# Six of sixteen feature blocks of a shift and scale moved from TensorE matmuls to VectorE dot products

## The chip, the cores and the metric

One core of one Trainium2 chip. Times are device microseconds (us) of one execution. The kernel before ran three times: 1409.14 us median, 1408.57 to 1409.15. Profile and trace come from one further execution.

## What is computed

One layer of a diffusion backbone for two groups of 128 tokens each (s = 0 prompt, s = 1 sample), model width 2048, feed-forward width 8192, all in float32. Cut to what matters here:

```python
def ada_mod(cvec, w_ada, b_ada):
    m = jax.nn.silu(cvec) @ w_ada + b_ada        # w_ada: 2048 x 12288
    return jnp.split(m, 6, axis=-1)
...
sh1, sc1, g1, sh2, sc2, g2 = ada_mod(c, w_ada, b_ada)
h = rms_norm(x, norm1_w) * (1 + sc1) + sh1       # then h @ w_in, two attentions, their branches, w_out
x = x + g1 * merged
h2 = rms_norm(x, norm2_w) * (1 + sc2) + sh2
x = x + g2 * (relu(h2 @ w_up) ** 2 @ w_down)
```

`c` is one vector per group, so the shift and scale are matrix-vector products with two vectors: 2048 inputs, 2048 outputs each. The change touches `sh2` and `sc2` alone. They are first needed when the second norm is applied, long after their weights can be had.

## The kernel before, in words

**Steps.** The big products run as 456 steps. A step is one weight tile of 512 KB (256 input rows by 512 columns, held as 128 partitions x 1024). For each step SyncE (SP) issues the load of `raw`; ScalarE (ACT) copies it to a rounded high part `wH` (L71, called from L193); VectorE (DVE) subtracts to get the low part `wL` (L206); TensorE (PE) does 12 matmuls of 128x512: high x high, low x high, high x low, for two 128-row slices and two token groups (L241 to L243, or L338 to L340 in the first 72 steps). A step's load is issued eight steps ahead (`LA` 4 and `RL` 4), its parts are made four steps ahead.

Steps 0 to 71 are the first nine column groups of `w_in`; 72 to 135 the eight gate groups; 136 to 167 the branches `w_br_a` and `w_br_b` (four units n of four plus four steps); 168 to 199 `w_out`; then up and down projections.

**The calendar.** The program is recorded step by step (`run`, L219 to L231), and each engine runs its own instructions strictly in that order. Ahead of step i come the loads due, then the preparation of step i + 4, then the step's matmuls, then whatever functions were put down for i with `at` or `ex`. So what stands behind step i on DVE comes after the `wL` of step i + 4, and the calendar fixes order and not time.

**What else DVE does around the change.** The gate g1 is computed on DVE: `gate_dve` (L949), eight SCALAR_TENSOR_TENSOR of 128x512 every five steps from step 84 to 161 (L953), closed four times by `spread`: ACT copies the sum (`SH`), DVE subtracts (`SL`, L75). Attention lies in steps 68 to 121: query and key norms, softmax sums and normalising on DVE, with small matmuls and transposes on PE (L518, L563, L610, L617, L621). At step 121 ACT applies six sigmoids of 128x1024 (L643). In a branch unit n, DVE multiplies and adds from PSUM (L669, L675, L676), and two steps after the unit PE transposes the result (`tT`, L658), so PE waits there for DVE's L676.

**The shift and scale of the second norm.** Sixteen feature blocks of 128 features. For block fb `pair_load` (L252) brings the shift and scale columns, 2 MB in four loads of 512 KB; `pair_mm` (L258, matmuls L265) does 16 float32 matmuls with the two conditioning vectors padded to 32 columns, in four column strips of the array. After each second block ACT copies the sums (`ada_evac`, L268) and one step later `ada_cols` (L274) turns them by four PE transposes (`ps_sel`, L281), and DVE adds strips and bias (L284 to L291). The blocks stand `SS_GAP` = 3.2 in units that make it 6.4 steps from block to block: steps 74, 80, 86, 93 and so on to 170.

**The pool.** Weights, parts and activations share one pool of `GEN` = 48 tiles of 128x1024 float32. A load into a tile waits until the last reader of the tile's former content is done.

Of the kernel before, what the change touches and what calls it, by code (L numbers as in the profile page):

```python
# [10 lines left out]
F32 = mybir.dt.float32  # L11
F32R = mybir.dt.float32r
BF16 = mybir.dt.bfloat16
AF = mybir.ActivationFunctionType
OP = mybir.AluOpType
AX = mybir.AxisListType

P = 128
D = 2048
KC = D // P  # L20
# [15 lines left out]
LA_OUT = {3: 3, 4: 2, 5: 2, 6: 2, 7: 2, 8: 2}  # L36
RL = 4
G1_AT, G1_GAP = 12, 5
SS_AT, SS_GAP = 2, 3.2
PIECES = [[2 * i, 2 * i + 1] for i in range(8)]  # L40
G2_GAP = 6
CHUNKS = [2, 2, 2, 2, 4, 4]
# [7 lines left out]
def tile_hybrid_step(ctx: ExitStack, tc: tile.TileContext, a):  # L50
    nc = tc.nc
    ctx.enter_context(tc.manual_schedule())
    cp = ctx.enter_context(tc.tile_pool(name="consts", bufs=1))
# [5 lines left out]
    act, dve, pe, pool, sync = nc.scalar, nc.vector, nc.tensor, nc.gpsimd, nc.sync  # L59
# [4 lines left out]
    def SM(n, name):  # L64
        return sp.tile([P, 32], F32, name=name, tag="s", bufs=14)[:, :n]

    def bank(name, pool_=None):
        return (pool_ or paux).tile([P, 512], F32, name=name, tag="b")
# [14 lines left out]
    baT = cols[:, 32:128].rearrange("p (a k) -> p a k", k=KC)  # L83
    nwT = cols[:, 128:160].rearrange("p (a k) -> p a k", k=KC)
# [87 lines left out]
    def load_at(i, fn):  # L172

        loads.append((i, len(loads), fn))
# [77 lines left out]
    def pair_load(box, nsub, fb):  # L252

        for q in range(4):
            box[fb, q] = G("araw")
            sync.dma_start(box[fb, q], a["w_pair"][nsub, fb][:, 1024 * q:1024 * q + 1024])

    def pair_mm(box, j, fb):  # L258

        if j == 0:  # L260
            box["ps"] = bank("ps_ada")
        for q in range(4):
            raw = box.pop((fb, q)).rearrange("p (k n) -> p k n", k=4)
            for k in range(4):
                pe.matmul(box["ps"][32 * k:32 * k + 32, 256 * j:256 * j + 256], cpad[:, 4 * q + k, :], raw[:, k, :],  # L265
                          start=j == 0 and q == 0, stop=j == 1 and q == 3, tile_position=(0, 32 * k))

    def ada_evac(box, n=512):  # L268
        box["S"] = sp.tile([P, 512], F32, name="S", tag="S", bufs=2)
        copy(box["S"][:, 0:n], box.pop("ps")[:, 0:n])  # L270

    mod = {}

    def ada_cols(box, nsub, k0, nk):  # L274

        if nsub not in mod:
            mod[nsub] = (cp.tile([P, KC, 2], F32, name=f"shT{nsub}"), cp.tile([P, KC, 2], F32, name=f"scT{nsub}"))
        shT, scT = mod[nsub]
        ps = bank("ps_sel")
        for i in range(2 * nk):  # L280
            pe.transpose(ps[:, i * P:(i + 1) * P], box["S"][:, i * P:(i + 1) * P], ident)  # L281
        ks = slice(k0, k0 + nk)
        t = SM(4 * nk, "t")
        dve.tensor_reduce(t.rearrange("p (i m) -> p i m", m=2),  # L284
                          ps[:, 0:2 * nk * P].rearrange("p (i j m) -> p i m j", j=4, m=32)[:, :, 0:2, :],
                          axis=AX.X, op=OP.add)
        tv = t.rearrange("p (k w s) -> p w k s", w=2, s=2)
        for w, dst in ((1, scT), (0, shT)):
            b = baT[:, 3 * nsub + w, ks].unsqueeze(2).to_broadcast([P, nk, 2])
            dve.tensor_tensor(dst[:, ks, :], tv[:, w], b, op=OP.add)  # L290
        dve.scalar_tensor_tensor(scT[:, ks, :], scT[:, ks, :], 1.0,  # L291
                                 nwT[:, nsub, ks].unsqueeze(2).to_broadcast([P, nk, 2]), op0=OP.add, op1=OP.mult)

    hH, hL = [None] * 4, [None] * 4

# [62 lines left out]
    def mod_pair(f):  # L358

        box, k0 = {}, 2 * f  # L360
        if f == 0:
            for j in range(2):
                pair_load(box, 0, j)
            for fn in [lambda: pair_mm(box, 0, 0), lambda: pair_mm(box, 1, 1), lambda: x_scale(0, 0, 2),
                       lambda: ada_evac(box), lambda: prep_hi(wsteps[0]), lambda: ada_cols(box, 0, 0, 2),
                       lambda: make_h(0, 2), lambda: prep_lo(wsteps[0], 0), lambda: split_h(0, 2),
                       lambda: prep_lo(wsteps[0], 1), lambda: x_scale(0, 2, 4)]:
                pre_at(0, fn)
            return
        i = ADA_AT[f]  # L370
        for j in range(2):
            load_at(i, lambda j=j: pair_load(box, 0, k0 + j))
            at(i, lambda j=j: pair_mm(box, j, k0 + j))
        at(i, lambda: ada_evac(box))
        at(i + 1, lambda: ada_cols(box, 0, k0, 2))
        at(i + 2, lambda: make_h(k0, 2))
        at(i + 3, lambda: split_h(k0, 2))
# [252 lines left out]
    t = 0  # L630
    for mix, s, g in [("A", 0, 0), ("A", 1, 0), ("A", 0, 1), ("A", 1, 1), ("B", 0, 0), ("B", 1, 0), ("B", 0, 1), ("B", 1, 1)]:
        need = [post_at["kvA", 0] + 6, post_at["qA", g] + 6] if mix == "A" else [
            post_at["kB", g] + 6, post_at["qB", g] + 6, end_of(("vB", g)) + 1]
        t = max([t + JOB_GAP] + need)
# [289 lines left out]
    def ex(i, fn):  # L924
        extra.setdefault(i, []).append(fn)
# [42 lines left out]

    end = sched_gate("g1", 2, s0 + G1_AT, G1_GAP)
    assert end <= br0 + 32, (end, br0)  # L970
    for c in range(8):
        box = {}
        for j in range(2):
            i = s0 + SS_AT + int((4 * c + 2 * j) * SS_GAP)
            load_at(i, lambda box=box, c=c, j=j: pair_load(box, 1, 2 * c + j))
            ex(i, lambda box=box, c=c, j=j: pair_mm(box, j, 2 * c + j))
        ex(i, lambda box=box: ada_evac(box))
        ex(i + 1, lambda box=box, c=c: ada_cols(box, 1, 2 * c, 2))
# [33 lines left out]
def _layout(x):  # L1012

    def tiles(w, n=512):
        k, m = w.shape
        return w.reshape(k // 256, 2, P, m // n, n).transpose(0, 3, 2, 1, 4).reshape(k // 256, m // n, P, 2 * n)

    out = {n: x[n] for n in ("x_prompt", "x_sample", "b_ada", "q_norm_a", "k_norm_a", "q_norm_b", "k_norm_b", "sink_a",
                             "cache_a_v", "cache_b_v")}
    for n in ("w_in", "w_br_a", "w_br_b", "w_out", "w_up", "w_down"):  # L1020
        out[n] = tiles(x[n][0])
    out["xT"] = np.stack([x["x_prompt"][0], x["x_sample"][0]]).reshape(2, P, 4, 4, P).transpose(2, 4, 3, 0, 1).reshape(4, P, 1024)
    rows = np.concatenate([x["c_ctx"], x["c"][0], x["b_ada"][0], x["norm1_w"][0], x["norm2_w"][0]])
    out["cols"] = rows.reshape(160, P).T
    ada = x["w_ada"][0]
    out["w_gate"] = np.stack([tiles(ada[:, p * D:(p + 1) * D]) for p in (2, 5)])
    pairs = []
    for p in (0, 3):
        w = ada[:, p * D:(p + 2) * D].reshape(KC, P, 2, KC, P)
        pairs.append(w.transpose(3, 1, 0, 2, 4).reshape(KC, P, KC * 2 * P))  # L1030
    out["w_pair"] = np.stack(pairs)
    out["cache_a_kT"] = x["cache_a_k"][0, 0].transpose(2, 1, 0)
    out["cache_b_kT"] = x["cache_b_k"][0, 0].transpose(2, 1, 0)
    q, k = np.arange(P)[:, None], np.arange(P)[None, :]
    rpb = x["rpb_b"][0]
    dr = k // GRID_W - q // GRID_W + rpb.shape[1] // 2
    dc = np.clip(k % GRID_W - q % GRID_W + rpb.shape[2] // 2, 0, rpb.shape[2] - 1)
    out["rpb_qk"] = rpb[:, dr, dc].transpose(1, 0, 2).reshape(P, NH * P)
    return {n: np.ascontiguousarray(v) for n, v in out.items()}
# [19 lines left out]
```

## Time and profile before

| | |
|---|---|
| median of 3 runs | 1409.14 us (1408.57 to 1409.15) |
| the profiled execution | 1408.84 us, of it the traced span 1407.1 us |
| PE busy | 1395.7 us, 99% of the span |
| DVE busy | 958.5 us, 68% |
| ACT busy | 640.6 us, 46% |
| HBM read | 346.28 MB, mean 249 GB/s |
| the block matmuls L265 (both norms) | 1024 records, 61.2 us |
| the preparation L206 on DVE | 455, mean 1221 ns |
| the gate's L953 on DVE | 256, mean 745 ns |

Busy time is time in which an instruction of the engine is in its recorded span. PE's spans overlap by design, so what a matmul costs is read from the distance of one start to the next. DVE's spans overlap by some 0.09 us where nothing waits; there too the start-to-start distance is the price. A wait is listed with the instruction that ended it.

### The profile page before, as it was taken

How to read it: one execution, taken by the hardware profiler on the slowest of the kernel's cores; microseconds unless marked ns; L12 is line 12 of the kernel's file. 1: busy time of each engine (PE TensorE's matmuls, PEld its weight loads, DVE VectorE, ACT ScalarE, POOL GpSimd, SP SyncE). 2: the span in 40 equal slices, each digit the busy share in tenths (PEclk: the TensorE clock that was granted, in tenths of full speed). 3: DMA queues.
4: the chain of work that ended last, by engine and by line, in shares of the span. 5: the costliest groups of instructions: out<-in, count | busy, mean ns of one | idle time of the engine just before them, and what ended most of it. 6: DMA issues, size and time to landing. Idle time of an engine off the chain costs nothing.

```text
span 1407.1 us, 18890 instructions
## 1 busy us (share of the span) xinstructions
PE 1395.7 (99%) x7118; PEld 1131.3 (80%) x7118; DVE 958.5 (68%) x1272; ACT 640.6 (46%) x846; POOL 48.7 (3%) x65
## 2 busy tenths in 40 slices
PE   8999999999999999999999999999999999999998
PEld 5777778877788777888888888888888888888887
DVE  3677766887776888755747778788754554544754
ACT  3633443365545543344644444444453543425431
POOL 0000010320000000000000000000000000000000
PEclk7999999999999999999999999999999999999999
DMA  9998876778788999975466766767666575565733
GB/s 379 399 364 326 318 290 226 251 250 292 242 288 294 392 339 346 326 232 173 154 222 220 256 226 230 250 239 269 216 203 195 179 209 186 175 209 167 224 109 114
DMA packets 98939, 350.94 MB, mean 249 GB/s; under 512 B 11616, under 2 KB 12640, under 8 KB 98848
## 3 DMA queue, kind: packets, MB, share of 16 engines
q1 hardware_dynamic: 97776, 348.31, 71.9%
q0 software_dynamic: 928, 1.34, 0.3%
q8 instruction: 56, 0.92, 0.3%
q14 instruction: 35, 0.29, 0.1%
q10 hardware_dynamic: 144, 0.08, 0.0%
HBM read 346.28 MB, written 3.41 MB: 249 GB/s over the span
## 4 chain that ended last, share of the span: by engine, by line
PE 98%; issue 1%; ACT 0%; DVE 0%; POOL 0%; POOLq 0%; ACTq 0%
PE acc L241 24%; PE acc L243 24%; PE acc L242 24%; PE acc L338 5%; PE acc L340 5%; PE acc L339 5%; PE ps_ada L265 4%; PE ps_T L658 1%; PE ps_S L563 1%; PE ps_g L940 1%; PE acc L742 1%; PE acc L741 1%; PE acc L740 1%; PE ps_sel L281 1%; PE acc L758 0%
## 5 line engine op out<-in xcount | busy, mean ns | idle before, releaser
L206 DVE TENSOR_TENSOR wL<-raw,wH 128x1024 fp32r<-128x1024 f32 x455 | 537.9, 1221 | 258.7 <-ACT wH L71 251.3
L71 ACT ACTIVATE wH<-raw 128x1024 fp32r<-128x1024 f32 x456 | 460.3, 1054 | 216.8 <-PE acc L243 62.9
L953 DVE SCALAR_TENSOR_TENSOR gacc<-araw,cpad,gacc 128x512 f32<-128x512 f32 x256 | 175.0, 745 | 0.0
L338 PE MATMUL acc<-wH,hH 128*128 128x512 f32 x288 | 114.1, 396 | 2.3 <-ACT hH L71 2.3
L340 PE MATMUL acc<-wH,hL 128*128 128x512 f32 x288 | 113.0, 393 | 0.0
L339 PE MATMUL acc<-wL,hH 128*128 128x512 f32 x288 | 112.8, 392 | 0.0
L241 PE MATMUL acc<-wH,hH 128*128 128x512 f32 x256 | 104.6, 409 | 0.0
L243 PE MATMUL acc<-wH,hL 128*128 128x512 f32 x256 | 100.1, 391 | 0.0
L242 PE MATMUL acc<-wL,hH 128*128 128x512 f32 x256 | 100.0, 390 | 0.0
L830 ACT ACTIVATE up<-acc 128x512 f32<-128x512 f32 x32 | 18.9, 590 | 153.2 <-PE acc L243 145.5
L901 DVE TENSOR_TENSOR dsum<-dsum,acc 128x512 f32<-128x512 f32 x48 | 32.4, 686 | 57.4 <-PE acc L243 57.4
L338 PEld LDWEIGHTS acc<-wH,hH 128*128 128x128 f32 x288 | 54.5, 189 | 16.4 <-issue 2.9
L340 PEld LDWEIGHTS acc<-wH,hL 128*128 128x128 f32 x288 | 54.5, 189 | 11.9 <-DVE hL L75 0.4
L339 PEld LDWEIGHTS acc<-wL,hH 128*128 128x128 f32 x288 | 54.4, 189 | 10.9
L265 PE MATMUL ps_ada<-araw,cpad 128*32 128x256 f32 x1024 | 61.2, 386 | 0.0
L241 PEld LDWEIGHTS acc<-wH,hH 128*128 128x128 f32 x256 | 48.1, 188 | 12.7 <-issue 3.4
L243 PEld LDWEIGHTS acc<-wH,hL 128*128 128x128 f32 x256 | 48.0, 188 | 10.4
L242 PEld LDWEIGHTS acc<-wL,hH 128*128 128x128 f32 x256 | 48.2, 188 | 9.9 <-issue 1.0
L265 PEld LDWEIGHTS ps_ada<-araw,cpad 128*32 128x32 f32 x1024 | 31.0, 111 | 27.4 <-issue 6.0
L71 ACT ACTIVATE S<-ps_ada 128x512 f32<-128x512 f32 x16 | 9.6, 601 | 92.8 <-PE ps_ada L265 92.8
L241 PE MATMUL acc<-wH,h21H 128*128 128x512 f32 x120 | 47.4, 395 | 0.0
L243 PE MATMUL acc<-wH,h20L 128*128 128x512 f32 x120 | 46.8, 390 | 0.0
(477 smaller groups left out, 2791.8 us busy)
## 6 DMA issues: line engine op xcount, KB each, us to landing
raw<-in_w_in SPq DMA_DIRECT2D x136, 512.0 KB, 5.6
araw<-in_w_pair SPq DMA_DIRECT2D x128, 512.0 KB, 7.5
raw<-in_w_up SPq DMA_DIRECT2D x128, 512.0 KB, 4.3
raw<-in_w_down SPq DMA_DIRECT2D x128, 512.0 KB, 4.2
araw<-in_w_gate SPq DMA_DIRECT2D x64, 512.0 KB, 5.6
raw<-in_w_out SPq DMA_DIRECT2D x32, 512.0 KB, 4.7
raw<-in_w_br_a SPq DMA_DIRECT2D x16, 512.0 KB, 6.8
raw<-in_w_br_b SPq DMA_DIRECT2D x16, 512.0 KB, 5.7
```

Of the source, the lines that this page charges most:

```text
L71: act.activation(out, in_, AF.Copy)
L206: dve.tensor_tensor(st["lo"], st["raw"], st["hi"].bitcast(F32), op=OP.subtract)
L241: pe.matmul(acc[tb], sh, wh[:, k, :], start=f, stop=False)
L242: pe.matmul(acc[tb], sh, wl[:, k, :], start=False, stop=False)
L243: pe.matmul(acc[tb], sl, wh[:, k, :], start=False, stop=l)
L265: pe.matmul(box["ps"][32 * k:32 * k + 32, 256 * j:256 * j + 256], cpad[:, 4 * q + k, :], raw[:, k, :], start=j == 0 and q == 0, stop=j == ...
L338: pe.matmul(acc[tb], sh, wh[:, k, :], start=kt == 0 and k == 0, stop=False)
L339: pe.matmul(acc[tb], sh, wl[:, k, :], start=False, stop=False)
L340: pe.matmul(acc[tb], sl, wh[:, k, :], start=False, stop=last and k == 1)
L830: act.activation(up_r[n][:, s, :], acc, AF.Relu)
L901: dve.tensor_tensor(dsum[n][:, s, :], dsum[n][:, s, :], acc[s], op=OP.add)
L953: dve.scalar_tensor_tensor(box["acc"][:, s, :], raw[:, j, :], cpad[:, 4 * kq + 2 * half + j, s:s + 1], box["acc"][:, s, :], op0=OP.mult, o ...
```

## The change

The last six feature blocks (10 to 15) of the second norm's shift and scale leave TensorE. Their weights are laid out by feature on the host (`w_adaT`: a partition is an output feature, the 2048 inputs lie along the row in two halves h). Both conditioning vectors are broadcast to all partitions, half by half (`crow`, `load_cond`), SiLU is applied there by ACT and DVE, and each output is a DVE `tensor_tensor_reduce`, 128x1024 float32, multiply and add, whose running start is the bias (first half) or the first half's result. In the recorded order each dot is two DVE instructions: the operation itself and one that writes the 128x1 result. Each weight tile serves two dots, one for each token group, two steps apart; a new tile comes every five steps from step 61 to 116 (first half) and 124 to 179 (second half). The ten blocks that stay on TensorE are spread 9.6 steps apart instead of 6.4 (`SS_GAP` 4.8): steps 74, 83, 93, 102, 112, 122, 131, 141, 150, 160.

```diff
-SS_AT, SS_GAP = 2, 3.2
+SS_AT, SS_GAP = 2, 4.8
+FB_DVE, DOT_AT, DOT_GAP = 10, 56, 5
...
+    def load_cond(h):
+        for s in range(2):
+            cB[s, h] = G(f"cB{s}")
+            sync.dma_start(cB[s, h], a["crow"][s:s + 1, 1024 * h:1024 * h + 1024].partition_broadcast(P))
+
+    def silu_cond(s, h):
+        t = G("sgB")
+        act.activation(t, cB[s, h], AF.Sigmoid)
+        dve.tensor_tensor(cB[s, h], cB[s, h], t, op=OP.mult)
+
+    def dot_load(box, fb, w, h):
+        box["raw"] = G("aT")
+        sync.dma_start(box["raw"], a["w_adaT"][w, fb - FB_DVE, h])
+
+    def dot(box, fb, w, h, s):
+        dst = mod[1][w][:, fb, s:s + 1]
+        out = box["raw"] if s else G("junk")
+        dve.tensor_tensor_reduce(out, box["raw"], cB[s, h], 1.0, dst if h else baT[:, 3 + w, fb:fb + 1], OP.mult, OP.add, dst)
...
+    i = DOT_AT
+    for h in range(2):
+        load_at(i - 1, lambda h=h: load_cond(h))
+        for s in range(2):
+            ex(i + s, lambda s=s, h=h: silu_cond(s, h))
+        for fb in range(FB_DVE, KC):
+            for w in range(2):
+                i += DOT_GAP
+                box = {}
+                load_at(i, lambda box=box, fb=fb, w=w, h=h: dot_load(box, fb, w, h))
+                for s in range(2):
+                    ex(i + 2 * s, lambda box=box, fb=fb, w=w, h=h, s=s: dot(box, fb, w, h, s))
+        i += 3
+    ex(i, dot_end)
...
-    for c in range(8):
+    for c in range(FB_DVE // 2):
```

`dot_end` is one small DVE operation that turns the six scales into norm weight times one plus scale. The line that created the result tiles is moved out of `ada_cols`, with no effect on the order.

More of the change, by code (lines that the diff above doesn't have):

```diff
@@ L274, in ada_cols @@
     def ada_cols(box, nsub, k0, nk):
-        if nsub not in mod:
-            mod[nsub] = (cp.tile([P, KC, 2], F32, name=f"shT{nsub}"), cp.tile([P, KC, 2], F32, name=f"scT{nsub}"))
         shT, scT = mod[nsub]
@@ L292, in ada_cols @@
                                  nwT[:, nsub, ks].unsqueeze(2).to_broadcast([P, nk, 2]), op0=OP.add, op1=OP.mult)
+    for n in range(2):
+        mod[n] = (cp.tile([P, KC, 2], F32, name=f"shT{n}"), cp.tile([P, KC, 2], F32, name=f"scT{n}"))
     hH, hL = [None] * 4, [None] * 4
@@ L970, in tile_hybrid_step, with dot_end @@
     assert end <= br0 + 32, (end, br0)
-    for c in range(8):
+    cB = {}
+    def load_cond(h):
[13 more added lines that the diff above has]
+        dve.tensor_tensor_reduce(out, box["raw"], cB[s, h], 1.0, dst if h else baT[:, 3 + w, fb:fb + 1], OP.mult, OP.add, dst)
+    def dot_end():
+        scT = mod[1][1][:, FB_DVE:KC, :]
+        nw = nwT[:, 1, FB_DVE:KC].unsqueeze(2).to_broadcast([P, KC - FB_DVE, 2])
+        dve.scalar_tensor_tensor(scT, scT, 1.0, nw, op0=OP.add, op1=OP.mult)
+    i = DOT_AT
[12 more added lines that the diff above has]
+    ex(i, dot_end)
+    assert i <= end_of(("out", 2)), (i, end_of(("out", 2)))
+    for c in range(FB_DVE // 2):
         box = {}
@@ L1031, in _layout @@
     out["w_pair"] = np.stack(pairs)
+    f0 = FB_DVE * P
+    out["w_adaT"] = np.stack([ada[:, p * D + f0:(p + 1) * D].reshape(2, 1024, KC - FB_DVE, P).transpose(2, 0, 3, 1) for p in (3, 4)])
+    out["crow"] = np.stack([x["c_ctx"], x["c"][0]])
     out["cache_a_kT"] = x["cache_a_k"][0, 0].transpose(2, 1, 0)
```

## The prediction

> **What bounds the kernel now.** I read the page's engine rows first, then the chain of work that ended last, then the groups by line. TensorE (PE) is busy for 99% of the span and the chain lies on it for 98%:
>
> ```profile
> PE 1395.7 (99%) x7118; PEld 1131.3 (80%) x7118; DVE 958.5 (68%) x1272; ACT 640.6 (46%) x846; POOL 48.7 (3%) x65
> PE 98%; issue 1%; ACT 0%; DVE 0%; POOL 0%; POOLq 0%; ACTq 0%
> L206 DVE TENSOR_TENSOR wL<-raw,wH 128x1024 fp32r<-128x1024 f32 x455 | 537.9, 1221 | 258.7 <-ACT wH L71 251.3
> L953 DVE SCALAR_TENSOR_TENSOR gacc<-araw,cpad,gacc 128x512 f32<-128x512 f32 x256 | 175.0, 745 | 0.0
> L265 PE MATMUL ps_ada<-araw,cpad 128*32 128x256 f32 x1024 | 61.2, 386 | 0.0
> ```
>
> So whatever leaves PE comes off the time, as long as the engine that takes it over keeps up in the stretch where it works. The 68% of VectorE (DVE) is a mean over unlike stretches and doesn't answer that.
>
> **What leaves PE.** The timeline of PE around one block of L265 and one set of four transposes (start, duration):
>
> ```profile
> 285.88 0.39 PE L243 MATMUL acc<-wH,hL 128*128 128x512 f32 x1
> 286.19 1.93 PE L265 MATMUL ps_ada<-araw,cpad 128*32 128x256 f32 x32
> 288.06 0.50 PE L241 MATMUL acc<-wH,hH 128*128 128x512 f32 x1
> 288.39 0.40 PE L242 MATMUL acc<-wL,hH 128*128 128x512 f32 x1
> 288.63 0.39 PE L243 MATMUL acc<-wH,hL 128*128 128x512 f32 x1
> ...
> 290.68 0.39 PE L243 MATMUL acc<-wH,hL 128*128 128x512 f32 x1
> 290.92 0.60 PE L281 MATMUL ps_sel<-ident,S 128*128 128x128 f32 x4
> ...
> 291.82 0.40 PE L243 MATMUL acc<-wH,hL 128*128 128x512 f32 x1
> ```
>
> Ordinary matmuls start 0.227 us apart (twelve make a step of 2.72). From 285.88 to 288.63 there are three such distances, 0.68, and the block: 2.75 - 0.68 = 2.07 us. Likewise 291.82 - 290.68 - 0.68 = 0.46 for the transposes. Other blocks give the same 2.07 to 2.08. Six blocks and three sets go: 6 x 2.07 + 3 x 0.46 = **13.8 us**, nearly 1%. The spreading of the other ten costs nothing by itself.
>
> **What DVE gets.** 48 dots of 128x1024, four multiplications like L206, one small operation; it loses three times some 0.5 us of small ones (L284 to L291). No row shows the dot. From below: a TENSOR_TENSOR of that size, 1.13 us from start to start (L206, three of them take 3.50 in the timeline at 457.43), if the result's write is free. From above, near: 1.22 in full, 0.06 for a scalar per partition (L953 at 745 ns against 692 for a TENSOR_TENSOR of the same 128x512, L708), 0.16 for the 128x1 instruction, as the small ones at L290 take, nothing overlapped: 1.44. From above, far: a multiplication and a TENSOR_REDUCE one after the other, 1.13 each (L483 takes 1213 ns), some 2.3. I take 1.13 + 0.06 + 0.10 = **1.29**, nearest to the row of the same shape and engine; 0.10 is the distance by which ACT's accumulator read at L579 moves its next instruction.
>
> [...]
>
> **Where DVE has room.** First half of the dots, steps 61 to 118: the table by stage gives DVE 176.17 us busy in the 223 us from 217 to 440, so 47 are free. 24 dots are 31 us, PE's way through is 6.7 us shorter, two multiplications 2.3: 40. Also `wL` is ready some 8 us before PE needs it there. I take this part as hidden. What hides it is DVE's idle time; without it each dot costs up to 1.29.
>
> First tight place, step 126. Before, the six sigmoids hold ACT up, and `wL` comes just in time (timeline of DVE):
>
> ```profile
> 445.46 2.73 DVE L953 SCALAR_TENSOR_TENSOR gacc<-araw,cpad,gacc 128x512 f32<-128x512 f32 x4
> 449.37 1.23 DVE L75 TENSOR_TENSOR SL<-gacc,SH 128x1024 fp32r<-128x1024 f32 x1 [1.18 <-ACT SH L71]
> 457.43 3.50 DVE L206 TENSOR_TENSOR wL<-raw,wH 128x1024 fp32r<-128x1024 f32 x3 [6.83 <-ACT wH L71]
> ```
>
> The first of these three ends at 458.66, PE starts step 126 at 459.06: 0.40 us of slack. The row of waits runs L953, SH, table load, six sigmoids, `wH`, `wL`. In the changed order two dots (2.58) and two multiplications (2.28) come ahead of that L953, small operations of 0.5 go, and PE gets there 2.07 sooner (two blocks between steps 118 and 125 become one). DVE's idle time between 436 and 445 is 0.36 + 1.25 + 0.26 = 1.87. So L953 ends 2.58 + 2.28 - 0.5 + 2.07 - 1.87 = 4.6 later as PE sees it. ACT's table load (1.28) now comes with the new sigmoids at step 119, while ACT waited 3.44 us for PE anyway, so 3.3 remain. PE waits 3.3 - 0.4 = 2.9.
>
> Second tight place, the branches, from there to the transposes of the last unit (L658), which start at 597.50:
>
> ```profile
> core 0: us, PE busy (x) PEld busy (x) DVE busy (x) ACT busy (x) POOL busy (x), PEclk, DMA share, GB/s
> 457.40:597.50 140.10, 140.10 (x796) 110.31 (x789) 120.76 (x156) 58.71 (x68) 1.92 (x3) 1.00 0.95 351
> ```
>
> DVE is at 86% here, against 68% overall. Its work up to the last L676 by start-to-start distances: 46 preparations at 1.135, 64 of L953 at 0.66, 30 operations of 128x512 at 0.6, two of L75 at 1.14, 1.0 of small ones: 115.8. Room: 140.1 - 115.8 = 24.3. In the changed order 18 dots stand in this stretch, 18 x 1.29 = 23.2; PE passes it two blocks and one set of transposes sooner, 4.6; and twice DVE waits for ACT between L953 and L75 (1.34 each, 2.7), which a late engine can't fill. With the 3.3 it is late by 3.3 + 23.2 + 4.6 + 2.7 - 24.3 = **9.5 us**. The 2.9 of step 126 are part of that, since time lost by PE is time gained by DVE. Behind the late L676 the transposes wait in PE's order, and every matmul of `w_out` behind them. From step 170 on DVE has room again (46.24 of 80 us busy from 600 to 680), too late to give PE anything back.
>
> **Edits that I cost at nothing.** Loads: 24 of 512 KB go, 24 of the same size come, one by one instead of four at a time, and four broadcast ones. DMA share is 0.95 in the tight stretch and bytes per step stay the same: 2 MB in 9.6 steps and 0.5 in 5 make 0.31 MB, 2 in 6.4 made 0.31. Today a weight load is issued 12 to 20 us before ACT reads it and lands in 5.6. ACT: four sigmoids, 4.2 us, against three copies of 0.6, with ACT at 58.71 of 140 in the tight stretch.
>
> **Sum.** 13.8 gained, 9.5 lost: 4.3. The profiled execution took 1408.84 (span 1407.1 and 1.7 around it), the median is 0.3 higher: **1404.5 us**.
>
> **Rivals.**
> 1. *DVE hides all.* For it: 68% mean, `wL` 8 us ahead. Against: the slack of 0.40 and of 3.3 us at two places. 1408.84 - 13.8 = 1395.0. With dots at 1.13 the 20 that count save 3.2 of the 9.5: 1401.3, still the forecast's kind. Chance 0.13 (1395 to 1398).
> 2. *Late loads.* Counted from first write to last read in the recorded order, 48 of the pool's 48 tiles are held at step 83, where it was 40, and loads for steps 89 to 91 then wait one step more; SP's queue is in order, so all behind them wait. Against: the 12 to 20 us. One step, 3.2 us with what lies between, at one or two such places on top of the forecast: 1407.5 to 1411. Chance 0.12.
> 3. *The dot costs 2.3 us* (the slower side). Place: the same two. First half: 24 x 2.3 + 2.3 + 6.7 = 64 against 47 of room and 8 of lead, 9 late; the branches another 18 x 1.0 over the 9.5. Loss 9 + 18 + 9.5 = 36 less 13.8: some 1431. It decides from the dot price at which the gain is gone: 4.3 over 20 dots, 0.21 more, 1.50 us. For it: no row has an accumulator on DVE. [...] Chance 0.16.
> 4. *It doesn't do what it says.* Against: the recorded order has 96 matmuls and 12 transposes fewer. 1409. Chance 0.02.
>
> Forecast: 0.57, from 1399 (dots near 1.13, less waiting) to 1407.5 (1.44: 20 x 0.15 = 3.0 more).
>
> **Chances.** Within 0.2% (2.8 us, about what a measurement here can tell from no change) is 1406.3 to 1412. Faster: 0.51 of the forecast and 0.13. Same: 0.06 of the forecast, 0.10 of rival 2, 0.02. Slower: 0.16 and 0.02 of rival 2. The range 1396.5 to 1411 leaves out rival 3, the ends of 1 and 2.
>
> **What would show it.** Right: L265 with 832 records; the dot's group with two instructions that take 1.29 us together from start to start; PE's waits for DVE at `ps_T` L658 (source L676) and for L206 near steps 126 and 156 to 170, some 9.5 us in all, all of it between 445 and 600; chain shares of DVE above 0%. Wrong: PE without gaps there (rival 1), loads ahead of the gaps (2), dots over 1.5 us (3), or waits already before 440, which I take as hidden.

## The result, and the profile after

The changed kernel takes **1431.43 us** (median; 1430.93 to 1435.95) against 1409.14: ratio 1.016, 95% interval 1.0147 to 1.0173. Slower by 22.3 us, where 4.6 us faster was forecast. The profiled execution is the longest of its four, 1435.95 (span 1434.2); some 3.6 us of that lie ahead of step 0, in code that the change doesn't touch, and are left out below.

The page after, the lines that answer to those of before:

```profile
PE 1396.0 (97%) x6914; PEld 1133.3 (79%) x6914; DVE 1017.8 (71%) x1361; ACT 643.1 (45%) x847; POOL 48.9 (3%) x65
PE 71%; DVE 4%; ACT 2%; issue 2%; DMA 0%; POOL 0%; ACTq 0%; DVEq 0%
L207 DVE TENSOR_TENSOR wL<-raw,wH 128x1024 fp32r<-128x1024 f32 x455 | 537.9, 1219 | 250.5 <-ACT wH L72 236.1
L955 DVE SCALAR_TENSOR_TENSOR gacc<-araw,cpad,gacc 128x512 f32<-128x512 f32 x256 | 174.9, 744 | 0.0
L266 PE MATMUL ps_ada<-araw,cpad 128*32 128x256 f32 x832 | 50.8, 394 | 0.0
```

PE lost 192 block matmuls (1024 to 832), just as forecast, and yet is busy as long as before; busy time doesn't tell why. DVE's mean is 71%, still far from full. The shares of the chain add up to 79% only: it is followed back from the end as far as the copy `T_kB` at 301.82 us and no further. So the 71% of PE are nine tenths of what was followed, against 98% before; DVE, 0% before, has 4%. What ended PE's waits says where to look (engine, line, what it waited for: total us, times, longest):

```profile
PE ps_sel L280 <- ACT S L72: 16.5, 4, 10.1
PE ps_S L565 <- ACT T_kB L72: 5.3, 1, 5.3
...
PE ps_PT L612 <- DVE prob L605: 1.4, 1, 1.4
PE acc L243 <- DVE wL L207: 1.4, 1, 1.4
...
PE ps_T L660 <- DVE g_gA L678: 0.7, 1, 0.7
```

The two waits that were forecast (`wL` L207, `ps_T` L660) are the small ones. The two largest are behind ACT, and neither was in the forecast. The largest, at step 123, on ACT:

```profile
471.91 1.06 ACT L72 ACTIVATE SH<-gacc 128x1024 fp32r<-128x1024 f32 x1 [5.72 <-DVE gacc L955]
472.87 3.88 ACT L645 ACTIVATE g_gB<-g_gB 128x1024 f32<-128x1024 f32 x4
476.66 1.99 ACT L645 ACTIVATE g_gA<-g_gA 128x1024 f32<-128x1024 f32 x2
478.55 1.04 ACT L72 ACTIVATE wH<-raw 128x1024 fp32r<-128x1024 f32 x1
479.49 0.57 ACT L72 ACTIVATE S<-ps_ada 128x512 f32<-128x512 f32 x1
```

and on PE:

```profile
480.12 1.12 PE L280 MATMUL ps_sel<-ident,S 128*128 128x128 f32 x4 [10.05 <-ACT S L72]
480.89 0.78 PE L242 MATMUL acc<-wH,hH 128*128 128x512 f32 x1
481.46 0.63 PE L243 MATMUL acc<-wL,hH 128*128 128x512 f32 x1
481.89 0.63 PE L244 MATMUL acc<-wH,hL 128*128 128x512 f32 x1
...
484.68 0.40 PE L242 MATMUL acc<-wH,hH 128*128 128x512 f32 x1
484.92 0.39 PE L243 MATMUL acc<-wL,hH 128*128 128x512 f32 x1
```

Three things are to be seen. The sums of two blocks (`S`) stand in ACT's order behind `SH` and the six sigmoids of step 121, because the new spacing closes a pair at step 122; before, pairs closed at 118 and 131. `SH` itself is late, since DVE finishes `gacc` late: dots and SiLU stand ahead of it. And behind the gap the matmuls start 0.43 us apart instead of 0.23, until 484.4, at a granted clock of 0.50: this wait costs PE some 2 us more than its own length.

**Accounts.** To place the loss I take the distance from start to start of each two matmuls, subtract the undisturbed one (0.227 for 512 columns, 0.11 for a transpose, 2.07 for a block), and sum by steps; gaps and the matmuls 0.43 us apart are both in it. The table gives it in us over the kernel before. The last column but one is 1409.1, less 13.8 where six blocks have left PE (all but e2), plus the sum; it meets each measured median within some 2 us, so no larger loss lies elsewhere. As 13.8 is taken away in it and is in the sum again, it is no test of the 13.8.

| kernel | 81-99 | 100-117 | 118-126 | 127-170 | sum | worked out | median |
|---|---|---|---|---|---|---|---|
| changed | 9.6 | 8.7 | 14.5 | 4.2 | 37.0 | 1432.3 | 1431.4 |
| e1 no dots | 1.2 | -0.2 | 7.6 | 0.0 | 8.6 | 1403.9 | 1404.3 |
| e2 dots only | 10.4 | 6.6 | 6.2 | 2.3 | 25.5 | 1434.6 | 1436.6 |
| e3 blocks 8 steps later | 14.4 | 7.6 | 11.8 | 5.3 | 39.1 | 1434.4 | 1435.1 |
| e4 old spacing | 10.4 | 6.6 | 6.1 | 12.4 | 35.5 | 1430.8 | 1431.1 |
| e5 first half early | 2.0 | -0.2 | 9.7 | 4.2 | 15.7 | 1411.0 | 1412.2 |
| e6 e5 and e3 | 3.6 | -0.1 | 5.6 | 5.3 | 14.4 | 1409.7 | 1410.1 |
| e7 e6, second half later | 3.6 | -0.1 | 1.5 | 3.8 | 8.8 | 1404.1 | 1404.3 |
| e8 e1 and e3 | 2.3 | -0.1 | 1.5 | 0.0 | 3.7 | 1399.0 | 1399.0 |
| e9 short dots | 6.0 | 3.6 | 11.2 | 0.9 | 21.7 | 1417.0 | 1416.7 |
| e10 one dot later | 9.9 | 7.5 | 14.2 | 4.2 | 35.8 | 1431.1 | 1431.5 |
| e11 second half split | 3.7 | -0.1 | 1.5 | 6.1 | 11.2 | 1406.5 | 1407.3 |
| e12 e9, result buffer | 5.0 | 3.5 | 10.8 | 0.8 | 20.1 | 1415.4 | 1416.9 |
| e13 e9, no loads | 1.4 | 1.7 | 11.0 | 0.1 | 14.2 | 1409.5 | 1409.9 |
| e14 split thin | 3.6 | -0.1 | 1.5 | 1.5 | 6.5 | 1401.8 | 1401.8 |

32.8 of the 37.0 us lie in steps 81 to 126, the attention and its end.

### The profile page after: what moved, and what is told of

Same layout as the page of the kernel before. It is cut to its first block, busy times and chain, and to the rows that moved or that the text cites. A ratio compares the mean times of both kernels' runs of the same rounds, so it can differ in the third digit from the quotient of the medians.

```text
span 1434.2 us, 18598 instructions
## 1 busy us (share of the span) xinstructions
PE 1396.0 (97%) x6914; PEld 1133.3 (79%) x6914; DVE 1017.8 (71%) x1361; ACT 643.1 (45%) x847; POOL 48.9 (3%) x65
## 4 chain that ended last, share of the span: by engine, by line
PE 71%; DVE 4%; ACT 2%; issue 2%; DMA 0%; POOL 0%; ACTq 0%; DVEq 0%
PE acc L242 21%; PE acc L243 21%; PE acc L244 21%; DVE wL L207 2%; PE ps_T L660 1%; ACT wH L72 1%; PE ps_ada L266 1%; PE acc L744 1%; PE acc L742 1%; PE acc L743 1%; PE ps_PT L612 0%; PE ps_S L565 0%; PE acc L760 0%; DVE gacc L955 0%; PE ps_g L942 0%
## 5 line engine op out<-in xcount | busy, mean ns | idle before, releaser
L207 DVE TENSOR_TENSOR wL<-raw,wH 128x1024 fp32r<-128x1024 f32 x455 | 537.9, 1219 | 250.5 <-ACT wH L72 236.1
L243 PEld LDWEIGHTS acc<-wL,hH 128*128 128x128 f32 x256 | 49.5, 193 | 10.4 <-issue 0.5
L266 PE MATMUL ps_ada<-araw,cpad 128*32 128x256 f32 x832 | 50.8, 394 | 0.0
L243 PE MATMUL acc<-wL,h21H 128*128 128x512 f32 x120 | 46.7, 389 | 0.0
L243 PE MATMUL acc<-wL,h20H 128*128 128x512 f32 x120 | 46.7, 389 | 0.0
```

The source lines that it names most:

```text
L207: dve.tensor_tensor(st["lo"], st["raw"], st["hi"].bitcast(F32), op=OP.subtract)
L243: pe.matmul(acc[tb], sh, wl[:, k, :], start=False, stop=False)
```

## Experiments

Two theories at first. A: the new spacing of the blocks is the cause (`S` behind `SH`). B: the dots are, by making DVE late.

**e1 and e2: each part alone.** e1 has the ten spread blocks and no dots:

```diff
-    i = DOT_AT
-    for h in range(2):
...
-    ex(i, dot_end)
+    for w in range(2):
+        dve.memset(mod[1][w][:, FB_DVE:KC, :], 1.0)
```

> Left out: the 48 dots, their 24 weight loads, the broadcast vectors and their SiLU; the shift and scale of blocks 10 to 15 are a constant, so the output is not the reference's. The ten PE blocks stay 9.6 steps apart. Theory A (the new spacing puts the copy of the sums, S, in ACT's order behind the gate's SH and, at step 121, behind six sigmoids, and PE's transposes wait for S): of the 13.8 us saved on PE some 9 are lost again at step 123 alone (S can come no earlier than about 458 on the clock of before, PE is there at about 451, and the matmuls after the gap run at half rate for some 2 us), 1403 to 1406. Theory B (all of the loss is VectorE being late because of the dots): 1395.3, no wait at the transposes.

Measured 1404.34, ratio 0.9955 (0.9938 to 0.9972), with a wait of 5.3 at `ps_sel` in step 123. As A has it: without any dot 8.6 of the 13.8 us are lost again, 7.6 of them in steps 118 to 126. How much of the 8.6 is the new places and how much PE's coming sooner, e1 doesn't tell; e8 below bears on it. Ten blocks at the old spacing without dots were not run. e2 has the dots and all sixteen blocks at their old places:

```diff
-SS_AT, SS_GAP = 2, 4.8
+SS_AT, SS_GAP = 2, 3.2
...
-        dst = mod[1][w][:, fb, s:s + 1]
+        dst = mod[0][w][:, fb, s:s + 1]
...
-    for c in range(FB_DVE // 2):
+    for c in range(8):
```

> All sixteen blocks stay on PE at their old steps, and the 48 dots with loads, broadcast and SiLU are added, their results going where nothing reads them. Theory A (spacing): no transposes behind SH, so the dots alone cost only what DVE is late near steps 126 and 166 to 169, less than the 9.5 us forecast since PE is slower by 13.8: 1411 to 1418. Theory B (dots): 1409.1 + 22.3 + 13.8 = 1445.

Measured 1436.62, 1.0179 (1.0155 to 1.0203). Here A fails: without any spacing the dots cost 25.5 us, where 2 to 9 were expected, though less than B's 36.

**e3 and e4: the blocks elsewhere.** In e3 `SS_AT` is 10 instead of 2, in e4 `SS_GAP` is 3.2 instead of 4.8.

> The changed kernel with its ten blocks eight steps later (82 instead of 74, the same 9.6 apart), so S is copied at steps 91, 110, 130, 149, 168, away from SH at 101, 121, 141, 161; this also gives T_kB another pool tile, long free. Theory A: the waits of 16.5 us at ps_sel and 5.3 at T_kB and the half-rate matmuls behind them (some 6) go: 1403, up to 1409 where DVE's lateness then shows elsewhere. Theory B: DVE is as late as before, the same time is lost at other places: 1427 to 1432.

> The changed kernel with the old spacing for its ten blocks: steps 74, 80, 86 to 131, S copied at 80, 93, 106, 118, 131. Theory A: as in the run with the shifted blocks, 1402 to 1409; PE has its blocks earlier, so less of them lies in the steps where DVE is tight, and DVE is later there by up to 4 us more. Theory B: 1427 to 1435.

Measured 1435.05, 1.0175 (1.0159 to 1.019), and 1431.07, 1.0147 (1.0126 to 1.0169). A fails on both. B's range has e4 in it; e3 lies 3 us above it. The waits at `ps_sel` shrink to 2.5 and 2.1, and others appear in their place, in e3 for instance:

```profile
PE acc L242 <- ACT wH L72: 4.4, 1, 4.4
PE ps_S L565 <- ACT T_kB L72: 3.8, 1, 3.8
PE ps_qT L520 <- ACT probT L72: 2.8, 1, 2.8
PE ps_g L942 <- ACT prob L577: 2.6, 1, 2.6
PE ps_sel L280 <- ACT S L72: 2.5, 2, 1.7
```

So the list of waits of the changed kernel named the nearest place where PE met a late DVE or ACT; with that place gone it meets them at the next. These five end on ACT; the next two, 2.2 each, end on DVE.

**e5 to e8: dots out of the attention.** That led to theory C: not the dots' number but their place inside the attention. If so, the same 24 dots must cost nothing ahead of step 72.

```diff
-    i = DOT_AT
     for h in range(2):
+        i = (20, 119)[h]
...
-                i += DOT_GAP
+                i += (4, 5)[h]
```

> The changed kernel with only the first half of the dots (24 of 48, with their loads and SiLU) moved ahead of the attention: from steps 61 to 118 to steps 24 to 70, every four steps instead of five; the second half (124 to 181) and the blocks stay. Theory C (in the attention, steps 81 to 126, each PE wait is a chain DVE, ACT, PE in strict order, and a dot ahead of a softmax operation delays all of it though DVE has idle time in the mean): the excess of PE's steps over their undisturbed length, 31 us there, falls to the 7 of the run without dots: 1431.4 - 24 = 1407. Theory D (48 dots on DVE cost the same wherever they stand, or their loads delay the weights, DMA being at 0.9 and more before 180 us): 1425 to 1432, with the waits now before step 72.

> As the run with the first half of the dots ahead of the attention, and in addition the blocks eight steps later, so that S is no longer copied behind SH and the sigmoids. Theory C: the remaining 7 to 9 us at the transposes go too; left are the second half's waits between steps 126 and 170, which were 4 to 7 us: 1395.3 + 5 = 1400, range 1397 to 1404. Theory D: 1427 to 1435.

> As the run before it, and in addition the second half of the dots nine steps later (133 to 190 instead of 124 to 181), so that four dots and two SiLU multiplications fewer stand ahead of step 126 and six more behind step 169. Theory C: 1 to 4 us less than the run before it, 1396 to 1400. If the transposes of the last branch unit hold against any delay, nothing.

> Left out: the dots and all that serves them, as in the first run without dots (six blocks' shift and scale are a constant); the ten blocks stand eight steps later, S away from SH. All theories: PE is rid of 13.8 us and nothing waits, 1409.1 - 13.8 = 1395.3. Above 1398 the term of 13.8 or the cause given for the 9 us of the first run is wrong.

e6 adds `SS_AT` 10 to e5; e7 has (20, 128) in place of (20, 119); e8 is e1 with `SS_AT` 10. Measured: e5 1412.15 (1.0018, 1.0006 to 1.003), e6 1410.10 (0.9997, 0.9986 to 1.0009), e7 1404.32 (0.9955, 0.994 to 0.9969), e8 1398.96 (0.9924, 0.9899 to 0.9949). Theory C holds in the main and D falls: e5's excess in steps 81 to 117 drops from 18.3 to 1.8. (Loads, tiles and SiLU moved with these dots; e9 to e13 take them apart.) e5 is still 5 us above C's 1407, with 9.7 left in steps 118 to 126 and 4.2 behind them. The 24 early dots with their 6 MB of loads cost nothing where they now stand. e6 came out 10 us above its expectation: 5.6 are still lost in steps 118 to 126, where SiLU and the first dots of the second half stand ahead of the gate, and 5.3 in the branches. e7, with the second half nine steps later, loses 1.5 and 3.8 there; it gained 5.8 on e6, more than the 1 to 4 expected, and ended 4 above its range. e8 missed its 1395.3 by 3.7, and passed by 1.0 the 1398 above which its expectation called the 13.8 or the cause wrong: PE without its blocks runs into the attention's own chain and into step 126 (`ps_o` waits 1.4 for `prob`, `wL` 0.8). That is the floor for these places of the blocks. So of e1's 8.6 the places make 4.9, as those go when the blocks stand eight steps later.

**e9 to e13: what of the dots costs.** e9 keeps every instruction and load and only shortens the dots.

```diff
-        dve.tensor_tensor_reduce(out, box["raw"], cB[s, h], 1.0,
+        dve.tensor_tensor_reduce(out[:, 0:32], box["raw"][:, 0:32], cB[s, h][:, 0:32], 1.0,
```

> Left out: of each dot all but the first 32 of its 1024 inputs, so each takes some 0.15 us of DVE instead of 1.28; the loads, the pool's tiles, the order of all instructions and the number of instructions stay those of the changed kernel. Theory C (DVE's time inside the attention's chains): as the first run without dots, 1404, up to 1409 with what the loads and the SiLU cost. Theory E (the 24 extra loads and the full pool, with T_kB in the tile of a dot's unused result): the waits stay, 1422 to 1430.

Measured 1416.73, 1.0044 (1.0031 to 1.0058): between both. The dots' time on DVE makes 15.3 of the 37.0 us; 13.1 more than e1 are left with hardly any dot time (0.17 us each from start to start). For those, e10 moves one dot (`i == 81`, s 0) by two steps, e12 gives the unused results a buffer of their own (`out = jk`), e13 also drops the 24 loads.

> The changed kernel with one dot of 48 moved two steps later: the one ahead of T_kB, whose pool tile had held that dot's unused result. T_kB now takes a tile freed by an earlier subtraction. If that tile was the cause of the wait of 5.3 us at step 82, it and some 2 us of half-rate matmuls go, 1424; if DVE is late there anyway, the wait shrinks by the dot's 1.28 or moves on to the next place, 1429 to 1431.

> Left out: all but 32 of each dot's 1024 inputs, as in the run with short dots; in addition the unused results go to a small buffer of their own and no longer take 24 tiles of the pool. If the result tiles made the 13 us that were left: 1404 to 1408. If the loads, the weight tiles or the SiLU did: 1414 to 1417.

> Left out: all but 32 of each dot's inputs, and the 24 weight loads with their tiles; the short dots multiply the broadcast vector with itself. SiLU, broadcast and the order stay. If loads and tiles made the 13 us: 1404 to 1408, what is left above 1404 being the SiLU at steps 119 and 120 (some 3.6 us at step 123). If the SiLU and the small instructions made them: 1414 to 1417.

Measured: e10 1431.45 (1.0152, 1.0129 to 1.0174), e12 1416.90 (1.0056, 1.0041 to 1.0071), e13 1409.93 (1.0006, 0.9997 to 1.0016). So loads with their tiles and the result tiles make 7.5 (e9 to e13); SiLU, the broadcast loads and the small instructions make 5.6 (e13 to e1), of these 3.4 at step 123, where the two new sigmoids and two multiplications stand ahead of `SH`. The result tiles alone make 1.6 in the table (e9 to e12) and nothing in the medians. How the pool acts is seen at step 82. In the changed kernel ACT's `T_kB` waits for the tile that a dot's unused result had held:

```profile
301.82 1.08 ACT L72 ACTIVATE T_kB<-ps_qT 128x512 f32<-128x512 f32 x2 [3.42 <-DVE shT L994]
```

With that dot moved (e10) the copy ahead of it waits for another tile, one being stored to the output:

```profile
297.09 1.06 ACT L72 ACTIVATE wH<-raw 128x1024 fp32r<-128x1024 f32 x1 [3.15 <-DMA out_new_b_k<-u_kB]
298.06 1.06 ACT L72 ACTIVATE T_kB<-ps_qT 128x512 f32<-128x512 f32 x2
```

and PE waits 5.0 instead of 5.3. My guess that this one tile was the cause is wrong; in both cases the tile that came next had been freed a moment before. Without the loads (e13) no wait for `T_kB` is left. Whether loads do harm beyond the tiles that they hold was not separated.

**e11 and e14: a better placing of the second half.** Both are e7 with other steps for the second half's tiles:

```diff
+        steps = iter(([*range(24, 72, 4)], [132, 139, 146, 153, 160, 167, 170, 173, 176, 179, 182, 185])[h])
...
-                i += DOT_GAP
+                i = next(steps)
```

(e14; e11 has 131, 134, 137, 140 and then 167 to 188 in threes.)

> As the run with the first half early and the second half late, but the second half's tiles stand at steps 131 to 140 (four) and 167 to 188 (eight) and none in the branches between. Theory C: the 4 us of waits at the branch transposes and at step 166 go, 1404.3 - 3.5 = 1400.8, and the run without dots at 1399 is the floor; range 1399.5 to 1402.5. If eight tiles in 22 steps are too many for DVE in w_out, waits appear at steps 170 to 199 and it is 1403 or more.

> First half of the dots early (steps 24 to 70), blocks eight steps later, second half thin in the branches and dense behind them: tiles at steps 132, 139, 146, 153, 160 and then every three steps from 167 to 185. DVE's room between steps 126 and 169 takes some 13 dots by the reckoning made ahead of the result, here are 10 or 11: waits at the branch transposes fall from 4 us to under 1, 1404.3 - 3.5 = 1401, floor 1399. If they don't fall, 1404 and the room is smaller than reckoned.

Measured: e11 1407.28 (0.9981, 0.9971 to 0.999), a miss; eight dots in twelve steps make PE wait 3.4 at `ps_T` in step 145, and behind the wait matmuls start 0.43 us apart instead of 0.23, which comes on top. e14 **1401.81** (0.9947, 0.9932 to 0.9962), faster than both kernels. Here are three stretches, roughly up to step 71, up to the tight place at step 126 (123 in the changed kernel) and up to step 170, first before (columns: busy us and instructions of each engine):

```profile
core 0: us, PE busy (x) PEld busy (x) DVE busy (x) ACT busy (x) POOL busy (x), PEclk, DMA share, GB/s
60.00:256.00 196.00, 196.00 (x1161) 154.68 (x1160) 143.20 (x208) 78.01 (x93) 10.92 (x13) 1.00 0.83 305
256.00:460.00 204.00, 203.87 (x1223) 162.02 (x1222) 158.70 (x290) 109.44 (x196) 24.49 (x24) 1.00 0.78 272
460.00:600.00 140.00, 140.00 (x778) 110.93 (x777) 119.42 (x156) 57.98 (x69) 1.92 (x3) 1.00 0.95 349
```

the changed kernel:

```profile
60.00:256.00 196.00, 196.00 (x1161) 154.69 (x1160) 149.51 (x210) 79.67 (x96) 8.97 (x11) 1.00 0.84 310
256.00:480.00 224.00, 200.83 (x1103) 159.60 (x1101) 185.02 (x333) 111.64 (x199) 26.64 (x27) 0.96 0.72 250
480.00:627.00 147.00, 143.62 (x732) 114.82 (x732) 139.05 (x190) 58.53 (x69) 1.91 (x3) 0.98 0.89 328
```

and e14:

```profile
60.00:256.00 196.00, 196.00 (x1161) 154.71 (x1160) 172.11 (x250) 81.59 (x97) 11.88 (x11) 1.00 0.89 332
256.00:460.00 204.00, 200.14 (x1105) 161.00 (x1104) 162.10 (x293) 109.76 (x197) 25.57 (x26) 1.00 0.74 254
460.00:600.00 140.00, 138.80 (x748) 110.64 (x748) 136.10 (x184) 61.65 (x72) 1.91 (x3) 1.00 0.93 345
```

Before step 72 DVE goes to 88% in e14 (172.11 of 196) and PE waits not at all. In the attention DVE is at 83% in the changed kernel (185.02 of 224), with 39 us of it idle, and PE stands still for 23 (224 less 200.83).

## Why the prediction was wrong, point by point

- **What bounds, and what leaves PE: right.** Steps 127 to 170 of e1 test the price: with three blocks and one set of transposes fewer, and no wait there, PE takes 134.58 us against 141.15 before, 6.57 less, where 3 x 2.07 + 0.46 = 6.67 were priced. A slip without effect: the sum leaves out its own last 0.3, since 1409.14 - 4.3 is 1404.8 and not 1404.5.
- **The dot's price: right.** 1.29 was taken, 1.20 measured from start to start as the timeline of DVE shows; the accumulator's read starts together with the next operation, so what it costs lies within the 1.20. On DVE, changed kernel:

```profile
300.44 1.28 DVE L994 CUSTOM_DVE_ANT_0 junk<-aT,cB,cols 128x1024 f32<-128x1024 f32 x1
301.64 0.08 DVE L994 DVE_READ_ACCUMULATOR2_ANT shT<- 128x1 f32 x1
301.64 1.22 DVE L207 TENSOR_TENSOR wL<-raw,wH 128x1024 fp32r<-128x1024 f32 x1
```

  So a dot takes 1.20 us where an L207 of the same size takes 1.13, and not the 2.3 of the far bound.
- **"I take this part as hidden": the step that failed.** Room of 47 us against 40 of work was a sum over 223 us. In steps 72 to 126 much of DVE's idle time is the waiting part of chains: DVE computes a maximum, ACT the exponential, PE a transpose, and so back, each engine in a fixed order. A dot ahead of the maximum delays the whole round, and the idle time behind it can't be used. In the changed kernel, on DVE, ACT and PE, with PE's step 101 starting at 376.34:

```profile
371.86 1.28 DVE L994 CUSTOM_DVE_ANT_0 junk<-aT,cB,cols 128x1024 f32<-128x1024 f32 x1
...
375.33 1.28 DVE L994 CUSTOM_DVE_ANT_0 aT<-aT,cB,cols 128x1024 f32<-128x1024 f32 x1
...
376.54 0.68 DVE L584 TENSOR_REDUCE mx<-ps_S 128x4 f32<-128x512 f32 x1
...
380.03 1.22 DVE L207 TENSOR_TENSOR wL<-raw,wH 128x1024 fp32r<-128x1024 f32 x1 [2.60 <-ACT wH L72]
...
390.50 1.06 ACT L72 ACTIVATE SH<-gacc 128x1024 fp32r<-128x1024 f32 x1 [7.24 <-DVE gacc L955]
...
393.04 1.11 PE L280 MATMUL ps_sel<-ident,S 128*128 128x128 f32 x4 [4.05 <-ACT S L72]
```

  The maximum (`mx`) starts 0.20 us behind the step's start; in e1 it starts 5.47 us ahead of it (361.81 against 367.28). Behind it DVE sits idle for 2.60, as the `wH` that it needs stands behind ACT's exponentials. Then `gacc`, `SH` and `S` are late, and PE waits 4.05 in step 103, where e1 has no wait. With the dots shortened (e9) the loss in that step falls from 5.0 to 2.0. The lead of `wL`, 8 us, covers one of PE's inputs and not `T_kB`, `prob` and `S`. Steps 81 to 126 lost 32.8 us, for which the forecast had 2.9. Of the 32.8 the dots' own time on DVE makes 12.0 (e9 has 20.8 there); the rest belongs to the next two points.
- **"The spreading of the other ten costs nothing by itself": wrong**, 4.9 of the 8.6 us of e1, by e8. The other 3.7 stay in e8; that PE, rid of six blocks, reaches other engines' results sooner is the likely reason. The blocks' matmuls are spread at no cost, but each pair brings a copy on ACT and transposes on PE, and these were moved behind `SH` and the sigmoids. The order of ACT was not read at the new places.
- **"Edits that I cost at nothing": wrong.** Loads and tiles 7.5; SiLU, broadcast loads and the small instructions 5.6. Rival 2 had the full pool at step 83, the right place, but saw late loads in it and priced 3.2; it was ACT's copies that waited.
- **The second tight place: too high.** The 6.6 us due there behind step 126 became 4.2, of which 1.8 are `S` behind `SH` at step 142. The waits that were forecast stand where they were forecast, but short: 1.36 for `wL` in step 166, 0.7 at `ps_T` in step 169. That PE's long waits ahead of it let DVE catch up is the likely reason, not tested by itself. e4, where PE arrives without blocks, lost 12.4 there, 5.8 of waits at `ps_T` among them: the mechanism is real.
- **Rival 3's 1431 is a chance hit.** It had the time and a wrong reason: the dot costs 1.20 and not 2.3.
- The forecast said that waits before 440 would prove it wrong. They did.

The 37.0 us in the order of the experiments: blocks gone and spread anew 8.6, SiLU, broadcast loads and small instructions 5.6, loads and tiles 7.5, the dots' DVE time 15.3. The shares depend on that order, as the causes meet at the same waits.

## What to carry to other kernels

Idle time of an engine counts as room only where nothing waits for its next instruction; in a chain that goes from engine to engine in a fixed order, added work costs up to its length, however idle the engine is in the mean: here the dots' own time cost 12.0 us in steps 81 to 126, with DVE at 83% in the attention. When steps are spread anew, read what stands ahead of each moved instruction on every engine, the copies and transposes above all. And a wait that is taken away proves its cause only if the time goes with it.

## What the runs showed of the hardware

- Behind some waits of PE, matmuls of 512 columns start 0.43 us apart instead of 0.23. In the changed kernel that follows waits of 4.05, 5.26 and 10.05 us, for 4.3 to 6.0 us from the end of the wait, at a granted clock of 0.50. By the distances it costs 2.1 to 2.9 us each, some 7 of the 37. In e1 a wait of 5.25 did the same, in e11 one of 3.42. Some shorter ones did it too: in e6 2.04 and 0.46 us in a row, in e4 1.83 and 0.67 within 2 us. Behind the changed kernel's waits of 1.36 and 1.56 the matmuls start 0.23 apart. From which length of wait on it happens was not measured.
- Ahead of step 0 the profiled execution took 28.6 us before and 32.1 in the changed kernel, though the work up to there is the same. Single runs of the kernel before, 1408.4 to 1412.9, scatter as widely. The cause was not sought.
